# A feed-forward down projection in fp32 pieces: all block products written out, against seven block products for eight on part of it

## The chip, the cores and the metric

The kernel runs on one core of a Trainium2 chip. The metric is the time on the device of one execution of the whole layer, in microseconds (us), as the median of several runs. The engines are named as in the profile: PE (TensorE, matmuls), DVE (VectorE), ACT (ScalarE), POOL (GpSimd) and SP (SyncE, here only an issuer of transfers).

## The reference, cut to what matters

The layer is a mixer, a cross attention and a feed-forward block, each between norms. The change is in the last product of the last block.

```python
def swiglu_ffn(h, w_gate_up, w_down):
    g, u = jnp.split(h @ w_gate_up, 2, axis=-1)
    return (jax.nn.silu(g) * u) @ w_down          # (512 x 2816) @ (2816 x 1024), float32

...
        h = rms_norm(x, ffn_norm_pre[l])
        y = swiglu_ffn(h, w_gate_up[l], w_down[l])
        x = x + rms_norm(y, ffn_norm_post[l])
```

## The kernel before

Every fp32 product is made of three matmuls in a one-pass format (fp32r): each operand is parted into a rounded piece and the rest, and `mm3` (L285 to L288) adds low times high, high times low and high times high. `split` (L164 to L171) parts one operand: ACT copies it into the rounded piece (L166), then DVE, or POOL if it is named, subtracts that from the operand (L167).

A scheduler orders each engine's instructions after the program is written; pools give out buffers and make a later user wait for the last reader of the earlier one. SP issues the loads, in order.

The gate and up products (`gate_up`, L1338) run for eleven column blocks of 256, `d` = 0 to 10, and already use seven block products for eight: `Blocks.sums` (L1276) makes the sums of activations, DVE those of the weights. Before block 1 it first finishes the block 0 (L1373 to L1380). POOL multiplies the gated halves into `Gf[d]` (L1366, L1370), which holds 256 rows of the inner dimension for all 512 tokens.

The down product (L1387 to L1422) runs over 22 tiles `k` of 128 inner rows. For each, SP has loaded 128 x 1024 weights, two tiles to a transfer (L1393). ACT and POOL part the activations (`gs`), ACT and DVE the weights (`hi`, `lo`), and PE runs 24 matmuls of 128 x 512: four token tiles `i`, two column halves `n`, three pieces. The eight results stay in the eight banks `bk_ff`. Weights and activations share the eight buffers of the pool `fw`, three to a tile. The last six tiles (`LAST`) are parted ahead and kept in `wd` buffers, so that PE can finish one token tile after the other, while the norm, the residual and the store of the one before run beside it.

Of the kernel before, what the change touches and what calls it, by code (L numbers as in the profile page):

```python
# [47 lines left out]
def hybrid_layer(ctx, tc, a, out):  # L48
# [124 lines left out]
    def kview(w):  # L173
        return w.rearrange("(k p) c -> p k c", p=P)
# [1033 lines left out]
    def pool(name, bufs, side="left"):  # L1208
        return ctx.enter_context(tc.tile_pool(name=name, bufs=bufs, side=side, reuse_waits="tile"))
# [8 lines left out]
    def wtile(shape=(P, 4, 256), name="wc"):  # L1218
        return fw.tile(list(shape), F32R, tag="wc", name=name)
# [12 lines left out]
    def ntile(shape, name="xn"):  # L1232
        return fn.tile(shape, F32, tag="xn", name=name, bufs=2)

    def gtile(shape=(P, 2, 512), name="gf"):
        return fg.tile(list(shape), F32, tag="gf", name=name)

    class Blocks:
# [33 lines left out]

        def sums(self):  # L1276
            q, r = self.whole
            s = [gtile((P, 2, 4, 128), name="as") for _ in range(2)]
# [26 lines left out]
    def halves(t):  # L1305
        return t.rearrange("p (z t) -> p z t", z=2)
# [22 lines left out]
    late.close()  # L1329
    fraw.append(pool("fr1", 2))  # L1330
    fa.append(pool("fa1", 4))
    fg = pool("fg", NF // 2)
    ft = pool("ft", 1)
    A.take(fa[1], "S2", "S1", "S3", "S4")

    Gf = {}

    def gate_up(d):  # L1338

        glo, ghi, ulo, uhi = load_gu(d)  # L1340
        X, Y = bank("sc", "bk_X"), bank("d", "bk_Y")
        product(X, weights(glo), "11", True)
        x1 = etile(name="x1")
        nc.scalar.activation(x1, X, AF.Copy)
        w21 = weights(ghi, nc.vector if d == 1 else nc.gpsimd)
        t1 = ft.tile([P, 4, 256], F32, tag="t1", name="t1")
        nc.vector.tensor_tensor(t1, ulo, glo, op=OP.subtract)
        nc.vector.tensor_tensor(ulo, uhi, ulo, op=OP.subtract)
# [16 lines left out]
        Gf[d] = gtile()  # L1365
        nc.gpsimd.tensor_tensor(Gf[d][:, :, 0:256], halves(x1), halves(u2), op=OP.mult)  # L1366
# [24 lines left out]
    for g in range(NF // 2):  # L1391
        raw = fraw[1 - g // 2 % 2].tile([P, 2, D], F32, tag="raw", name="raw")
        nc.sync.dma_start(raw, wd[:, 2 * g:2 * g + 2, :])  # L1393
        for q in range(2):
            k = 2 * g + q
            gs = wtile((P, 2, 512), name="gs")
            if k >= NF - LAST:
                w2 = fa[len(tail) >= 3].tile([P, 2, D], F32R, tag="A", name="wd")
                hi, lo = w2[:, 0, :], w2[:, 1, :]
            else:  # L1400
                hi, lo = wtile((P, D), name="whi"), wtile((P, D), name="wlo")
            split(gs[:, 0], gs[:, 1], Gf[g][:, q], nc.gpsimd)
            split(hi, lo, raw[:, q, :])
            if k >= NF - LAST:
                tail.append((k, gs, hi, lo))
                continue
            for i in range(NT):
                t = slice(128 * i, 128 * i + 128)
                for n in range(2):
                    c = slice(512 * n, 512 * n + 512)  # L1410
                    mm3(bk[i][n], gs[:, 0, t], gs[:, 1, t], hi[:, c], lo[:, c], k == 0, False)
    for i in range(NT):
        t = slice(128 * i, 128 * i + 128)
        for n in range(2):
            c = slice(512 * n, 512 * n + 512)
            for k, gs, hi, lo in tail:
                mm3(bk[i][n], gs[:, 0, t], gs[:, 1, t], hi[:, c], lo[:, c], False, k == NF - 1)
        xo = ntile([P, D], name="xo")
        post_second(post_first(bk[i][0], g_post3, etile), bk[i][1], g_post3, res(i), xo, etile)
        for n in range(2):  # L1420
            c = slice(512 * n, 512 * n + 512)
            nc.sync.dma_start(out[0, 128 * i:128 * i + 128, c], xo[:, c])  # L1422
# [29 lines left out]
```

## Time and profile before

| what | value |
|---|---|
| median of 3 runs | 838.19 us (837.92 to 840.44) |
| the profiled execution, its own time | 842.27 us |
| span in its profile, first to last instruction | 840.5 us |
| PE busy, share of the span | 818.5 us, 97% |
| DVE, ACT, POOL busy | 535.3 us, 424.8 us, 290.8 us |
| mean granted clock of TensorE | 0.99 |

The span is what the profile's rows add up to; the profiled execution's own time is 1.8 us above it. The share of a busy engine is an average over stages with different limits, so that what matters is read from the stage of the change. Matmuls overlap in the record: one of 128 x 512 shows a length of 0.39 us, while the next starts 0.23 us later, and the distance from start to start is what a matmul costs.

### The profile page before, as it was taken

What the parts mean: (1) busy time and instruction counts of PE and PEld (TensorE: products, weight loads), DVE (VectorE), ACT (ScalarE), POOL (GpSimd) and SP (SyncE); (2) the same over time, 40 slices, a digit from 0 to 9 for tenths busy, and PEclk for the clock granted to TensorE, in tenths of its full rate; (3) what the DMA queues carried; (4) which work ended last, traced back from release to release, by engine and by line L of the source; (5) the groups of instructions that cost most, each with busy time, mean ns of one, the idle gap of its engine ahead of it and who ended that gap; (6) DMA issues with size and microseconds to landing.
All of it is one profiled execution on the core that took longest, in us unless ns stands there. A gap on an engine that the chain in (4) does not pass through costs nothing.

```text
span 840.5 us, 12639 instructions
## 1 busy us (share of the span) xinstructions
PE 818.5 (97%) x4838; PEld 706.2 (84%) x4838; DVE 535.3 (64%) x936; ACT 424.8 (51%) x840; POOL 290.8 (35%) x218
## 2 busy tenths in 40 slices
PE   8999989989999999999999999999999999999997
PEld 6877858876689878778888899999999999888885
DVE  5766684897889735743553779877888885124323
ACT  5535566768768643633543465444444444334311
POOL 1015331455537343501420101444444444323320
PEclk9999989999999999999999999999999999999999
DMA  8238312221102431243323034333333323222102
GB/s 249 75 106 259 110 52 81 82 70 63 63 14 89 150 102 51 100 150 101 101 101 100 10 117 152 119 109 106 114 103 103 102 101 101 101 101 100 51 26 76
DMA packets 67763, 83.18 MB, mean 99 GB/s; under 512 B 4368, under 2 KB 53873, under 8 KB 67702
## 3 DMA queue, kind: packets, MB, share of 16 engines
q1 hardware_dynamic: 64574, 77.97, 28.8%
q10 hardware_dynamic: 3128, 4.40, 1.7%
q8 instruction: 38, 0.62, 0.3%
q14 instruction: 23, 0.19, 0.1%
HBM read 80.24 MB, written 2.12 MB: 98 GB/s over the span
## 4 chain that ended last, share of the span: by engine, by line
PE 88%; DVE 7%; ACT 2%; issue 2%; DMA 1%; POOL 0%; SPq 0%; DVEq 0%; ACTq 0%; POOLq 0%
PE bk_dT L286 6%; PE bk_dT L287 6%; PE bk_dT L288 6%; PE bk_X L1300 5%; PE bk_X L1301 5%; PE bk_X L1302 5%; PE bk_ff L287 5%; PE bk_ff L288 5%; PE bk_ff L286 5%; PE bk_pv L1026 3%; PE bk_dN L287 3%; PE bk_dN L286 3%; PE bk_dN L288 3%; PE bk_Z L1300 2%; PE bk_Z L1301 2%; PE bk_Z L1302 2%
## 5 line engine op out<-in xcount | busy, mean ns | idle before, releaser
L166 ACT ACTIVATE whi<-raw 128x1024 fp32r<-128x1024 f32 (+1 forms) x80 | 76.8, 967 | 72.0 <-PE bk_dT L286 35.3
L167 DVE TENSOR_TENSOR wlo<-raw,whi 128x1024 fp32r<-128x1024 f32 x43 | 56.7, 1322 | 85.9 <-PE bk_ff L287 43.0
L167 POOL TENSOR_TENSOR wlo<-raw,whi 128x1024 fp32r<-128x1024 f32 x21 | 50.3, 2396 | 121.4 <-ACT whi L166 119.5
L166 ACT ACTIVATE wh<-raw 128x1024 fp32r<-128x1024 f32 x64 | 67.2, 1057 | 49.3 <-PE bk_X L1300 17.7
L167 POOL TENSOR_TENSOR wl<-raw,wh 128x1024 fp32r<-128x1024 f32 x19 | 55.4, 2917 | 97.3 <-ACT wh L166 69.9
L286 PE MATMUL bk_dT<-hTh,wlo 128*128 128x512 f32 x192 | 77.6, 404 | 1.2 <-DVE wlo L167 0.9
L287 PE MATMUL bk_dT<-hTl,whi 128*128 128x512 f32 x192 | 76.9, 400 | 0.0
L288 PE MATMUL bk_dT<-hTh,whi 128*128 128x512 f32 x192 | 76.4, 398 | 0.0
L167 DVE TENSOR_TENSOR wl<-raw,wh 128x1024 fp32r<-128x1024 f32 x45 | 65.7, 1465 | 9.3 <-ACT wh L166 9.3
L1301 PE MATMUL bk_X<-A,wh 128*128 128x256 f32 x192 | 54.5, 284 | 1.0 <-DVE A L167 1.0
L167 POOL TENSOR_TENSOR gs<-gf,gs 128x512 fp32r<-128x512 f32 x22 | 32.4, 1477 | 65.9 <-ACT gs L166 65.9
L1300 PE MATMUL bk_X<-A,wl 128*128 128x256 f32 x192 | 54.4, 283 | 0.4 <-ACT A L166 0.4
L1302 PE MATMUL bk_X<-A,wh 128*128 128x256 f32 x192 | 54.3, 283 | 0.0
L287 PE MATMUL bk_ff<-wlo,gs 128*128 128x512 f32 x128 | 49.8, 389 | 0.0
L288 PE MATMUL bk_ff<-whi,gs 128*128 128x512 f32 x128 | 49.6, 389 | 0.0
L1300 PE MATMUL bk_X<-AS,wl 128*128 128x256 f32 x160 | 45.6, 285 | 2.4 <-ACT u L1355 2.3
L286 PE MATMUL bk_ff<-whi,gs 128*128 128x512 f32 x128 | 47.4, 389 | 0.0
L996 POOL TENSOR_SCALAR s<-s,acf 128x128 f32<-128x128 f32 (+3 forms) x32 | 36.3, 1146 | 26.7 <-PE bk_tr L1011 15.9
L286 PEld LDWEIGHTS bk_dT<-hTh,wlo 128*128 128x128 f32 x192 | 36.6, 191 | 10.4 <-DVE wlo L167 2.1
L1302 PE MATMUL bk_X<-AS,wh 128*128 128x256 f32 x160 | 44.9, 281 | 0.0
L1300 PE MATMUL bk_Z<-AS,wl 128*128 128x256 f32 x160 | 44.9, 280 | 0.0
L1301 PE MATMUL bk_X<-AS,wh 128*128 128x256 f32 x160 | 44.8, 280 | 0.0
(376 smaller groups left out, 2527.9 us busy)
## 6 DMA issues: line engine op xcount, KB each, us to landing
raw<-in_w_gate_up_dram SPq DMA_DIRECT2D x22, 1024.0 KB, 5.5
raw<-in_w_down_dram SPq DMA_DIRECT2D x11, 1024.0 KB, 4.9
raw<-in_w_xkv_dram SPq DMA_DIRECT2D x8, 1024.0 KB, 5.3
raw<-in_w_in_dram SPq DMA_DIRECT2D x7, 1024.0 KB, 5.2
raw<-in_w_out_dram SPq DMA_DIRECT2D x4, 1024.0 KB, 5.0
raw<-in_w_xq_dram SPq DMA_DIRECT2D x4, 1024.0 KB, 5.2
raw<-in_w_xo_dram SPq DMA_DIRECT2D x4, 1024.0 KB, 5.0
raw<-in_w_in_dram SPq DMA_DIRECT2D x6, 512.0 KB, 4.8
```

Source lines behind the costliest of these rows:

```text
L166: first = nc.scalar.activation(hi, src, AF.Copy)
L167: second = (eng or nc.vector).tensor_tensor(lo, src, hi.bitcast(F32), op=OP.subtract)
L286: nc.tensor.matmul(o, lhsT=wl, rhs=xh, start=start, stop=False)
L287: nc.tensor.matmul(o, lhsT=wh, rhs=xl, start=False, stop=False)
L288: return nc.tensor.matmul(o, lhsT=wh, rhs=xh, start=False, stop=stop).ins
L996: ENG[on].tensor_scalar(s[:, 0:n], s[:, 0:n], c, None, op0=OP.mult)
L1026: nc.tensor.matmul(o, lhsT=v, rhs=pTs[br][q][:, j], start=(br, j, q) == mms[0], stop=(br, j, q) == mms[-1])
L1300: nc.tensor.matmul(o, lhsT=wl[:, k, c], rhs=A.hi(n, k), start=st, stop=False, skip_group_check=True)
L1301: nc.tensor.matmul(o, lhsT=wh[:, k, c], rhs=A.lo(n, k), start=False, stop=False, skip_group_check=True)
L1302: nc.tensor.matmul(o, lhsT=wh[:, k, c], rhs=A.hi(n, k), start=False, stop=stop and k == 3, skip_group_check=True)
```

## The change

The 2816 inner rows are seen as eleven pairs of tiles. Three pairs (`D0` = 3) are multiplied as before, into eight banks. For the other eight pairs the product is cut in two by two by two blocks: token halves 1 and 2, inner halves 1 and 2 (the two tiles of each pair), column halves 1 and 2. Seven block products replace eight: 11·11, 21·11, 12·21, 11·11, 12·22, 21·12 and 22·11 (activation block, weight block), where the blocks are overwritten in place by sums between the products. Each product takes four steps (`PAIRS`), and each step 12 matmuls of 128 x 512.

- The sums of activations (`gsum`) are eight DVE instructions of 128 x 1024.
- The first weight sum (11 += 12) is four DVE instructions (`wsum`, `dma=False`). The others (12 += 22, 11 += 22, 11 += 21) are twelve transfers of 512 KB, issued by POOL, which add what they read from the weights in memory onto a block that is already in the core (`accum_op=OP.add`).
- In the steps both lower pieces are made by DVE (before, POOL made those of the activations). `in_turn` keeps the order of the steps on ACT and DVE.
- Five additions of banks to kept results (`plus`, `kept`) are new, and the norm sums its halves as they come. Before the last product the rows 0 and 1 of token tiles are finished; only the rows 2 and 3 come after it.
- The activations of all blocks are now two tiles `G`, a part of which serves `sums` as its scratch.

```diff
-    wd = kview(a["w_down"][0])
-    bk = [[bank(t, "bk_ff") for t in ts] for ts in (("d", "d"), ("tr", "tr"), ("b", "b"), ("b", "b"))]
-    LAST = 6
...
-            split(gs[:, 0], gs[:, 1], Gf[g][:, q], nc.gpsimd)
-            split(hi, lo, raw[:, q, :])
...
-                    mm3(bk[i][n], gs[:, 0, t], gs[:, 1, t], hi[:, c], lo[:, c], k == 0, False)
...
+    def wsum(o, x, pairs, dma=True):
+        for q in pairs:
+            if dma:
+                last = nc.gpsimd.dma_start(block(o, *q), of_weights(x, *q), accum_op=OP.add)
+            else:
+                last = nc.vector.tensor_tensor(block(o, *q), block(o, *q), block(x, *q), op=OP.add)
+        return last.ins
+    def gsum(o, x, y, op, minus=False):
+        for q in FOURS:
+            o_, x_, y_ = (quarter(n, *q) for n in (o, x, y))
+            if minus:
+                nc.vector.scalar_tensor_tensor(o_, x_, -1.0, y_, op0=OP.mult, op1=op)
+            else:
+                nc.vector.tensor_tensor(o_, x_, y_, op=op)
+    def pieces(g, w, q, big=None):
...
+            wh, wl = wtile((P, 2, 512), name="whi"), wtile((P, 2, 512), name="wlo")
+        gs = wtile((P, 2, 2, 256), name="gs")
+        with in_turn():
+            split(gs[:, 0], gs[:, 1], quarter(g, *q))
+            parted.append(split(wh, wl, block(w, *q)))
+        return gs, wh, wl
...
+    def times(b, i, parts, q, start, stop):
+        gs, wh, wl = parts
+        t = slice(128 * i, 128 * i + 128)
+        for k in range(2):
+            d = q[0] + k
+            mm3s(b[i], gs[:, 0, k, t], gs[:, 1, k, t], wh[:, k], wl[:, k], start and d == D0, stop and d == ND - 1)
+    def one_pair(b, g, w, start, q):
+        parts = pieces(g, w, q)
+        for i in range(2):
+            times(b, i, parts, q, start, True)
...
+    c12, c22 = kept(X, pair_of("c12")), kept(Y, pair_of("c22"))
+    c21 = kept(V, [G[0][:, z, 0:2, :].rearrange("p d t -> p (d t)") for z in range(2)])
+    for q in PAIRS:
+        one_pair(X, "11", "11", True, q)
+        wsum("11", "12", [q], dma=False)
+    c11 = kept(X, pair_of("c11"))
+    gsum("21", "21", "22", OP.subtract)
+    last = wsum("12", "22", PAIRS[0:2])
+    for q in PAIRS:
+        one_pair(Y, "21", "11", True, q)
+        with tc.issue_after(last):
+            last = wsum("11", "22", [q])
+    plus(c22, Y)
+    gsum("11", "21", "11", OP.subtract)
+    with tc.issue_after(last):
+        last = wsum("12", "22", PAIRS[2:])
+    whole_product(Z, "12", "21", False)
+    plus(c11, Z)
+    whole_product(X, "11", "11", False)
+    plus(c12, X, OP.subtract)
+    gsum("21", "22", "11", OP.subtract, True)
+    gsum("12", "12", "11", OP.add)
+    with tc.issue_after(last):
+        wsum("11", "21", PAIRS)
+    whole_product(Y, "12", "22", False)
+    plus(c12, Y)
+    whole_product(X, "21", "12", False)
+    plus(c22, X, OP.subtract)
+    for i in range(2):
+        out_half(i, 1, c12[i], c12[i], True)
+        out_half(i, 0, c11[i], c11[i])
+        out_row(i)
+    TAIL = 2
...
+    for n, q in enumerate(PAIRS):
+        late = n >= len(PAIRS) - TAIL
+        parts = pieces("22", "11", q, fa[0] if late else None)
...
+    for i in range(2):
+        out_half(2 + i, 1, c22[i], c22[i], True)
+    for i in range(2):
+        for q, parts in tail:
+            times(X, i, parts, q, False, True)
+        nc.vector.tensor_tensor(c21[i], X[i], c21[i], op=OP.add)
+        out_half(2 + i, 0, c21[i], etile(name="yo"))
+        out_row(2 + i)
```

Three places of the order are needed below. The first is DVE in the down product. Before, from the last gate and up block on, its rows are the lower pieces of weights alone (`wlo`, and `wd` for the last six tiles):

```order
L1364 TENSOR_TENSOR u_7452<-u_7452,bk_Z 128x512
L167 TENSOR_TENSOR wlo<-raw,whi 128x1024 x10
L167 TENSOR_TENSOR wd<-raw,wd 128x1024 x2
L167 TENSOR_TENSOR wlo<-raw,whi 128x1024
L167 TENSOR_TENSOR wd<-raw,wd 128x1024 x2
```

With the change, these rows follow each other from the second step of the first block product to the first step of the second (`gs_7830` and `wlo_7829` are the second step's lower pieces, `gs_7898` and `wlo_7897` those of the second product's first; L1435 is a weight sum, L1444 a sum of activations):

```order
L167 TENSOR_TENSOR gs_7830<-gf_5118,gs_7830 128x512
L1435 TENSOR_TENSOR raw_7576<-raw_7576,raw_7578 128x1024
L167 TENSOR_TENSOR wlo_7829<-raw_7576,whi_7828 128x1024
L1444 TENSOR_TENSOR gf_5118<-gf_5119,gf_5118 128x1024
L167 TENSOR_TENSOR gs_7850<-gf_5118,gs_7850 128x512
L167 TENSOR_TENSOR wlo_7849<-raw_7582,whi_7848 128x1024
L1435 TENSOR_TENSOR raw_7576<-raw_7576,raw_7578 128x1024
L167 TENSOR_TENSOR gs_7870<-gf_5118,gs_7870 128x512
L167 TENSOR_TENSOR wlo_7869<-raw_7582,whi_7868 128x1024
L1435 TENSOR_TENSOR raw_7582<-raw_7582,raw_7580 128x1024
L167 TENSOR_TENSOR gs_7898<-gf_5119,gs_7898 128x512
L1444 TENSOR_TENSOR gf_5118<-gf_5119,gf_5118 128x1024
```

The next row is `wlo_7897`. Between the lower pieces of one step and the next now stand sums that the list before does not have.

The second place is DVE again, from the last step of the sixth product to the first of the seventh (`wlo_8282` and `wlo_8335`; L1522 finishes token row 1, L1491 takes the sixth product out of the bank into which the seventh adds):

```order
L167 TENSOR_TENSOR wlo_8282<-raw_7580,whi_8281 128x1024
L167 TENSOR_TENSOR gs_8336<-gf_5119,gs_8336 128x512
L1522 SCALAR_TENSOR_TENSOR xo_8318<-c12_7799,rs_r_8327,xin_113 128x512
L1522 SCALAR_TENSOR_TENSOR xo_8318<-c11_7889,rs_r_8327,xin_113 128x512
L167 TENSOR_TENSOR wlo_8335<-raw_7576,whi_8334 128x1024
L167 TENSOR_TENSOR gs_8355<-gf_5119,gs_8355 128x512
L1491 TENSOR_TENSOR c22_7802<-c22_7802,bk_ff_7592 128x512
```

Before, nothing read a bank in the middle of the down product; the finishing rows stood behind the last lower pieces.

The third is DVE between the gate and up blocks 0 and 1, as one piece of the difference (`A_4828` and `A_4829` are the lower pieces of the block 21 of the last token tile, in two halves, `A_4825` that of the block 22; L1279 to L1288 are sums of `Blocks.sums`, and `AS` their lower pieces):

```order
+L1279 TENSOR_TENSOR gf<-aw 128x512
+L1280 TENSOR_TENSOR gf<-gf,aw 128x512
+L1285 TENSOR_TENSOR aw<-aw 128x512
+L1288 TENSOR_TENSOR aw<-aw,gf 128x512
+L167 TENSOR_TENSOR AS_5114<-gf,AS_5114 128x4x128
+L167 TENSOR_TENSOR AS_5115<-gf,AS_5115 128x4x128
 L167 TENSOR_TENSOR A_4828<-bk_pn,A_4826 128x2x128
+L167 TENSOR_TENSOR AS_5116<-aw,AS_5116 128x4x128
+L1378 TENSOR_TENSOR gf<-s_5218,bk_Y 128x2x256
 L167 TENSOR_TENSOR A_4825<-bk_pn,A_4825 128x4x128
+L167 TENSOR_TENSOR AS_5117<-aw,AS_5117 128x4x128
 L167 TENSOR_TENSOR A_4829<-bk_pn,A_4827 128x2x128
```

Half of the sums, which stood behind the pieces of the last token tile, now stand ahead of and among them.

## Rows read from the trace of the kernel before

**Rows 1.** The page: the span, and busy time of each engine.

```profile
span 840.5 us, 12639 instructions
PE 818.5 (97%) x4838; PEld 706.2 (84%) x4838; DVE 535.3 (64%) x936; ACT 424.8 (51%) x840; POOL 290.8 (35%) x218
```

**Rows 2.** Busy time by stretch, and the columns.

```profile
core 0: us, PE busy (x) PEld busy (x) DVE busy (x) ACT busy (x) POOL busy (x), PEclk, DMA share, GB/s
711.00:834.40 123.40, 123.33 (x554) 101.85 (x552) 37.57 (x39) 37.69 (x57) 34.28 (x28) 1.00 0.21 73
500.00:700.00 200.00, 197.59 (x1645) 196.02 (x1645) 166.44 (x131) 98.41 (x124) 89.79 (x37) 1.00 0.32 106
```

**Rows 3.** Tile `bk_ff`: one of the three matmul rows of the first sixteen tiles.

```profile
L286 PE MATMUL bk_ff<-whi,gs x128: 387/389/398, 711.0 to 800.3; 128*128 128x512 f32 x128
```

**Rows 4.** Timeline of PE: starts of two matmuls of the down product, 19 steps apart.

```profile
738.65 0.39 PE L287 MATMUL bk_ff<-wlo,gs 128*128 128x512 f32 x1
...
742.95 0.39 PE L288 MATMUL bk_ff<-whi,gs 128*128 128x512 f32 x1
```

**Rows 5.** Waits in the down product, 710 to 800.5 us, longest first.

```profile
POOL gs L167 <- ACT gs L166: 59.1, 17, 6.4
DVE wlo L167 <- PE bk_ff L287: 43.0, 10, 8.2
```

**Rows 6.** Timeline of DVE: instructions that follow each other without a wait.

```profile
500.27 0.69 DVE L1281 TENSOR_TENSOR as<-as,aw 128x512 f32<-128x512 f32 x1
500.87 0.69 DVE L1286 TENSOR_TENSOR aw<-aw 128x512 f32<-128x512 f32 x1
...
517.35 3.43 DVE L167 TENSOR_TENSOR wl<-raw,wh 128x1024 fp32r<-128x1024 f32 x1
...
521.84 1.21 DVE L167 TENSOR_TENSOR wl<-raw,wh 128x1024 fp32r<-128x1024 f32 x1
522.98 1.21 DVE L1348 TENSOR_TENSOR raw<-raw 128x1024 f32<-128x1024 f32 x1
```

**Rows 7.** Timeline of POOL beside the longest of these.

```profile
516.31 3.39 POOL L167 TENSOR_TENSOR wl<-raw,wh 128x1024 fp32r<-128x1024 f32 x1 [27.36 <-DVE x L1351]
```

**Rows 8.** Timeline of ACT: one step's two upper pieces in the down product.

```profile
722.81 0.63 ACT L166 ACTIVATE gs<-gf 128x512 fp32r<-128x512 f32 x1 [4.38 <-PE bk_ff L288]
723.35 1.05 ACT L166 ACTIVATE whi<-raw 128x1024 fp32r<-128x1024 f32 x1
```

**Rows 9.** Timeline of PE: a matmul behind a wait, and the next two.

```profile
485.02 0.39 PE L1301 MATMUL bk_X<-A,wh 128*128 128x256 f32 x1 [0.97 <-DVE A L167]
485.24 0.28 PE L1302 MATMUL bk_X<-A,wh 128*128 128x256 f32 x1
485.36 0.28 PE L1300 MATMUL bk_X<-A,wl 128*128 128x256 f32 x1
```

**Rows 10.** Timeline of DVE and PE between gate and up blocks 0 and 1.

```profile
496.64 0.42 DVE L167 TENSOR_TENSOR A<-bk_pn,A 128x256 fp32r<-128x256 f32 x1 [2.64 <-ACT A L166]
...
498.13 0.28 PE L1300 MATMUL bk_X<-A,wl 128*128 128x256 f32 x1
```

**Rows 11.** Timeline of the end, from the last matmul on.

```profile
833.93 0.39 PE L288 MATMUL bk_ff<-wd,gs 128*128 128x512 f32 x1
834.36 0.60 ACT L259 ACTIVATE pn<-bk_ff 128x512 f32<-128x512 f32 x1 [3.39 <-PE bk_ff L288]
...
835.98 1.41 DVE L283 SCALAR_TENSOR_TENSOR xo<-yo,rs_r,xin 128x512 f32<-128x512 f32 x2 [0.20 <-POOL rs_r L280]
```

**Rows 12.** Transfers: KB of one, median us from issue to landing.

```profile
raw<-in_w_down_dram SPq DMA_DIRECT2D x11, 1024.0 KB, 4.9
raw<-in_w_in_dram SPq DMA_DIRECT2D x6, 512.0 KB, 4.8
xin<-in_x_dram SPq DMA_DIRECT2D x4, 512.0 KB, 3.6
raw<-in_w_in_dram SPq DMA_DIRECT2D x2, 304.0 KB, 7.7
```

More of the change, by code (lines that the diff above doesn't have):

```diff
@@ L1331, in hybrid_layer @@
     fa.append(pool("fa1", 4))
-    fg = pool("fg", NF // 2)
+    fg = pool("fg", 2)
     ft = pool("ft", 1)
     A.take(fa[1], "S2", "S1", "S3", "S4")
-    Gf = {}
+    G = [fg.tile([P, 2, NF // 2, 256], F32, tag="gf", name="gf") for _ in range(2)]
     def gate_up(d):
@@ L1412, in hybrid_layer @@
[L1412 to L1422, printed above, removed]
+    wd = a["w_down"][0].rearrange("(d h p) c -> p h d c", h=2, p=P)
@@ new lines, in hybrid_layer, with of_weights, load_b, load_plain @@
+    ND, D0 = NF // 2, 3
+    B = {}
+    def of_weights(name, d0, d1):
+        c = 512 * int(name[1]) - 512
+        return wd[:, int(name[0]) - 1, d0:d1, c:c + 512]
+    def load_b(name, g, home, tag):
+        t = B[name, g] = home.tile([P, 4, 512], F32, tag=tag, name="raw")
+        nc.sync.dma_start(t, of_weights(name, D0 + 4 * g, D0 + 4 * g + 4))
+    def load_plain(home):
+        raw = home.tile([P, 2, D], F32, tag="raw", name="raw")
+        nc.sync.dma_start(raw, wd[:, :, len(plain), :])
+        plain.append(raw)
@@ new lines, in hybrid_layer, with block, quarter @@
+    plain = []
+    load_plain(fraw[1])
+    load_plain(fraw[1])
+    load_plain(fraw[0])
+    load_b("11", 0, fraw[0], "raw")
+    load_b("12", 0, fa[0], "A")
+    load_b("12", 1, fa[0], "A")
+    load_b("11", 1, fa[1], "A")
+    load_b("21", 0, fa[1], "A")
+    load_b("21", 1, fa[1], "A")
+    load_b("22", 0, fa[1], "A")
+    load_b("22", 1, fraw[1], "raw")
+    def block(name, d0, d1):
+        g, k = (d0 - D0) // 4, (d0 - D0) % 4
+        return B[name, g][:, k:k + d1 - d0]
+    def quarter(name, d0, d1):
+        return G[int(name[0]) - 1][:, int(name[1]) - 1, d0:d1, :]
@@ new lines, in hybrid_layer, with in_turn @@
+    parted = []
+    def in_turn():
+        behind = ExitStack()
+        for ins in parted[-1] if parted else ():
+            behind.enter_context(tc.issue_after(ins))
+        return behind
+    def pieces(g, w, q, big=None):
+        if big:
+            W = big.tile([P, 2, 2, 512], F32R, tag="A", name="wd")
+            wh, wl = W[:, 0], W[:, 1]
+        else:
+            wh, wl = wtile((P, 2, 512), name="whi"), wtile((P, 2, 512), name="wlo")
[4 more added lines that the diff above has]
+        return gs, wh, wl
@@ new lines, in one_pair, with whole_product, plus, kept @@
+    def one_pair(b, g, w, start, q):
+        parts = pieces(g, w, q)
+        for i in range(2):
+            times(b, i, parts, q, start, True)
+    def whole_product(b, g, w, start):
+        for q in PAIRS:
+            one_pair(b, g, w, start, q)
+    def plus(t, b, op=OP.add):
+        for i in range(2):
+            nc.vector.tensor_tensor(t[i], t[i], b[i], op=op)
+    def kept(b, t):
+        for i in range(2):
+            nc.scalar.activation(t[i], b[i], AF.Copy)
+        return t
+    def pair_of(name):
+        return [etile(name=name) for _ in range(2)]
@@ new lines, in hybrid_layer, with out_half, out_row @@
+    outs, sq = {}, {}
+    def out_half(i, n, src, t, eps=False):
+        if i not in outs:
+            outs[i] = ntile([P, D], name="xo"), {}
+        xo, ts = outs[i]
+        sq[i, n] = small([P, 1], "ss%d" % n, 4)
+        square_sum(sq[i, n], src, xo[:, 512 * n:512 * n + 512])
+        if eps:
+            nc.vector.tensor_scalar(sq[i, n], sq[i, n], EPS, None, op0=OP.add)
+        nc.vector.tensor_tensor(t, src, g_post3[n], op=OP.mult)
+        ts[n] = t
+    def out_row(i):
+        xo, ts = outs[i]
+        e, r = small([P, 1], "rs_e", 4), small([P, 1], "rs_r", 4)
+        nc.gpsimd.tensor_tensor(e, sq[i, 0], sq[i, 1], op=OP.add)
+        nc.gpsimd.tensor_tensor(r, e, mhalf[:, 0:1], op=OP.pow)
+        for n in (1, 0):
+            c = slice(512 * n, 512 * n + 512)
+            nc.vector.scalar_tensor_tensor(xo[:, c], ts[n], r, res(i)[:, c], op0=OP.mult, op1=OP.add)
+            nc.sync.dma_start(out[0, 128 * i:128 * i + 128, c], xo[:, c])
@@ new lines, in hybrid_layer @@
+    X, Y, V, Z = ([bank(t, "bk_ff") for t in ts] for ts in (("d", "d"), ("tr", "tr"), ("b", "b"), ("b", "b")))
+    home = {"12": X, "22": Y, "21": V, "11": Z}
+    for d in range(D0):
+        ops = []
+        for z in range(2):
+            hi, lo = wtile((P, D), name="whi"), wtile((P, D), name="wlo")
+            gs = wtile((P, 2, 2, 256), name="gs")
+            with in_turn():
+                for u in range(2):
+                    split(gs[:, 0, u], gs[:, 1, u], G[u][:, z, d, :], nc.gpsimd if d else None)
+                parted.append(split(hi, lo, plain[d][:, z, :]))
+            ops.append((hi, lo, gs))
+        for zs in ((0,), (1,)) if d < D0 - 1 else ((0, 1),):
+            for name in ("12", "22", "21", "11"):
+                u, c = int(name[0]) - 1, 512 * int(name[1]) - 512
+                for i in range(2):
+                    t = slice(128 * i, 128 * i + 128)
+                    for z in zs:
+                        hi, lo, gs = ops[z]
+                        mm3s(home[name][i], gs[:, 0, u, t], gs[:, 1, u, t], hi[:, c:c + 512], lo[:, c:c + 512],
+                             d == z == 0, d == D0 - 1 and z == 1)
@@ L1425 @@
+    for i in range(2):
+        for q, parts in tail:
+            times(X, i, parts, q, False, True)
+        nc.vector.tensor_tensor(c21[i], X[i], c21[i], op=OP.add)
+        out_half(2 + i, 0, c21[i], etile(name="yo"))
+        out_row(2 + i)
 _INS = ['x', 'mem', 'rel_bias', 'mix_norm_pre', 'w_in', 'cmp_pos_k', 'cmp_pos_v', 'cmp_w1_k', 'cmp_w2_k', 'cmp_w1_v',
```

44 lines of the change are left out of this document (18 added, 26 removed).

## The prediction, made before the changed kernel was run

> **What bounds the kernel now.** I began with the page. The span is 840.5 us and PE is busy for 818.5 of it [rows 1], so PE bounds the kernel almost everywhere, and a matmul taken out is worth its time wherever PE does not start to wait. Then I read the down product by stretch: from 711.0 to 834.4 us PE is busy for 123.33 of 123.40 us, at the full granted clock (1.00, which is the 2.4 GHz level), while DVE, ACT and POOL have about 35 us of work each [rows 2]. Its matmuls are those of the down product (22 tiles of 24, 528, in three lines of which one has 128 for the first sixteen tiles [rows 3]) and the last of the gate's. The distance between starts gives the price: from 738.65 to 742.95 there are 19 steps of 0.226 us [rows 4]. The whole stage gives the mean: 24 gate matmuls of 0.12 us [rows 9] are 2.9, and (123.3 - 2.9)/528 = 0.228 us. The waits say how much room there was: in the down product DVE's lower pieces waited 43.0 us for PE to free a buffer, POOL's 59.1 us for ACT [rows 5]. Nobody waited on DVE. So the stage before is PE and nothing else, and the question is whether the other engines still keep up when DVE gets twice its work.
>
> **Fewer matmuls.** Three plain pairs are 3 x 48 = 144 matmuls, seven products of 4 steps of 12 are 336; together 480, 48 fewer: 48 x 0.228 = -10.9 us.
>
> **DVE's load in the steps.** A step gives PE 12 x 0.2265 = 2.72 us. From start to start, 512 elements on DVE take 0.60 and 1024 take 1.14 us [rows 6]; a scalar_tensor_tensor of 512 takes 0.70 (1.41 for two) [rows 11]. A step needs gs and wlo, 1.74 us; 28 steps are 48.7. To that come four weight sums (4.6), eight sums of activations (about 9.7), ten additions of banks (6.0) and the finishing of two rows (about 5): 74 us, against 28 x 2.72 = 76 us of PE. That is 97%, but no stall in itself: between 500 and 700 us DVE was busy 166 of 200 us and PE still 197.6 [rows 2]. What counts is where the work bunches, since the buffers let DVE run only about two steps ahead. ACT's two pieces of a step, about 0.55 + 1.0 [rows 8], fit into 2.72.
>
> **First bunch, products 1 to 2.** From the second step's gs to the second product's wlo, DVE's order has 4 gs (2.4), 4 wlo (4.56), 3 weight sums (3.4) and 2 sums of activations (2.3): 12.7 us. It can start about 0.2 us after PE enters product 1 (the buffers of the last plain pair are freed then), so wlo_7897 is ready 12.9 us in. PE wants it after four steps and one matmul, 10.9 + 0.2 = 11.1. Stall 1.8 us, and some 0.5 more in the next two steps, which have the remaining sum: **+2.3**. Its bounds: 0, if DVE gets half a step further ahead; 3.5, if DVE takes its whole 1.21 and 0.69 us per instruction, not the pitch.
>
> **Second bunch, start of product 7.** Its bank is read by L1491 first. Behind wlo_8282 stand gs, two L1522, wlo, gs and the first L1491: 0.60 + 1.4 + 1.14 + 0.60 + 0.68 = 4.4 us, while PE has about 2.5 us of its step left. Stall 1.9, and 0.2 for the second half-bank: **+2.1** (0 to 3).
>
> **Restarts.** The first matmul behind a wait costs more: 0.22 us to the next start where the next has 0.12 [rows 9]. About nine waits of this kind (products 1, 2 and 7): **+0.9** (0.3 to 1.5).
>
> **Gate and up, block 0 to 1.** DVE was idle for 2.64 us ahead of A [rows 10]; the four sums and two pieces now put there are 6 x 0.60 = 3.6 us, so it is 1.0 later. Two more pieces and L1378 (1.8) then stand ahead of A_4829; before, it was there by about 498.0 (PE goes on at 498.13), so it now comes at about 500.8. PE's first matmul with it stands 14 rows behind the one at 498.13, so at 498.13 + 14 x 0.12 = 499.8: **+1.0** (0 to 1.5). The hidden part is hidden by PE's own 14 matmuls alone.
>
> **The end.** Before, ACT squares the bank itself 0.43 us after the last matmul's start [rows 11]. Now a DVE addition (0.69) stands between: **+0.75**. The rest of the chain has the same length, and only two rows' finishing, not four, stands after the last product, as before one row.
>
> **The adding transfers.** Twelve of 512 KB, issued by POOL; no row of before shows one. The nearest rows are loads of 512 KB by SP: 3.6 and 4.8 us, and of 1024 KB (as an addition also reads what it changes): 4.9; the slowest kind took 7.7 for 304 KB [rows 12]. They go one after another by their blocks: the first can start about 3 us into product 1, the last is needed about 73 us in, before product 7's last step. So they are hidden up to 70/12 = 5.8 us each; beyond that each further us costs 12. I take 4.8, like the 512 KB loads of weights: hidden, **0**. Bounds 3.6 (0) and 7.7 (+22). The Trainium skill, "DMA: Bandwidth & Descriptors", section on the anatomy of one DMA on the gpsimd path, gives 2.0 us + bytes/436e3 for such a transfer; my estimate from it is 3.2 us, so by that too the sum stays the same. No run here shows it yet. The loads themselves (8 of 1 MB for the blocks, three for the plain pairs) are the 11 of before and go through the same queue, whose share of the engines was 0.21 [rows 2].
>
> **Sum.** -10.9 + 2.3 + 2.1 + 0.9 + 1.0 + 0.75 = -3.85. The span goes from 840.5 to 836.6, and with the 1.8 around it the execution from 842.27 to 838.4. The profiled execution stood 4.1 us above the median of 838.19; I take that off and forecast a median of **834.3**. By the terms' bounds without the transfers it is 829 to 838. What this measurement can tell from no change is 0.3%, so under 835.7 is faster and over 840.7 slower.
>
> **Rivals.**
> *The adding transfers are too slow.* From 6.4 us each (12 x 6.4 - 70 = 6.8 us of waits, more than the 6.4 that separate forecast and bound), the kernel is slower; 6.5 us gives 842, 7.7 gives 856. For it: an addition has to read as much again, and small loads took up to 7.7. Against it: 1 MB loads in the same stage took 4.9, and the engines are 80% idle [rows 2, 12]. ACT's upper pieces in product 4 or 7 would wait for a transfer. Chance 0.18.
>
> *DVE becomes the bound.* At 1.21 and 0.69 per instruction its 74 us are 79 to 80, above PE's 76, and what PE loses grows by about 3 us to 837.5 (836 to 841). For it: only three per cent of room. Against it: the rows show the pitch held over instructions that follow each other, and the steps are such instructions. Chance 0.14.
>
> *POOL and DVE hold each other up.* One DVE lower piece of 1024 took 3.43 us instead of 1.21 where a POOL lower piece took 3.39 at the same time [rows 6, 7]. If writing out a transfer did the same to DVE, twelve times 2.2 us = 26 us would fall on an engine with 2 us of room: 855 to 860. Against it: POOL no longer makes pieces in the steps, which is the one thing that the row shows to collide; issuing a transfer moves no tile through POOL. Chance 0.05. The Trainium skill, "SBUF — State Buffer", section "Who interferes with whom", has a DVE instruction with two inputs from SBUF contend with a GpSimd one that reads it, and holds (as an inference) that writing descriptors is not stopped by it; with the first the rows agree. By its "DVE blocks DMA" trap a DVE instruction of another kind does stop it: if it held here, the first four transfers would wait for DVE's first pause, about 22 us into product 1, and the limit of 5.8 us would fall to 4.2, at which 4.8 us each would cost 7 us: 841. It is inside this chance.
>
> *The stalls are absent.* If PE never waits in the steps or between the blocks: -10.9 + 0.9 + 0.75, 829. For it: DVE was idle 70% of the stage and PE waited for nobody [rows 2]. Against it: the counts above, which hold at any start. Chance 0.08.
>
> **How the numbers follow.** The forecast has what is left, 0.55, with a range of its own of 831 to 837.5. Of it some 0.5 lies under 835.7; with the absent stalls and the lower part of the dear DVE, faster has 0.60. Same has 0.17 (the upper edge of the forecast, most of the dear DVE), slower 0.23 (transfers 0.18, collisions 0.05). The range of 829 to 846 leaves out the slow end of the transfers, the collisions and half of the absent stalls, together under 0.2.
>
> **What would show it.** 480 matmuls on `bk_ff`, 0.226 to 0.23 from start to start. PE's longest waits on DVE's wlo at the first step of product 2 (near 1.8 us) and on L1491 at the first of product 7 (near 2). DVE's rows 1.14 and 0.60 apart; if they are dearer, or stretched where POOL issues, the second or third rival holds. Transfers that land in under 5.8 us one after another, and no piece of ACT waiting for one; if ACT waits, it is the first rival. A wait of about 1 us of PE near 499.8 us, and 0.75 us more from the last matmul to the end. Wrong it would be above all through the price of an adding transfer, which nothing here shows.

## The result

The changed kernel takes 846.33 us (median of 5 runs, 844.47 to 849.37) against 839.66 us of the kernel before (5 runs): 1.0092 times, 95% interval 1.0075 to 1.0109. It is 6.7 us slower, where 3.9 us less had been forecast, and just above the upper end of the range (846). Its profiled execution has this page (to read beside [rows 1]):

```profile
span 845.3 us, 12704 instructions
PE 807.3 (96%) x4790; PEld 694.6 (82%) x4790; DVE 584.2 (69%) x1004; ACT 449.4 (53%) x878; POOL 280.8 (33%) x216
```

PE has 48 matmuls and 11.2 us of work less, as counted. So the time went into waits. Busy time by stretch of the down product (columns as in [rows 2]) shows where:

```profile
core 0: us, PE busy (x) PEld busy (x) DVE busy (x) ACT busy (x) POOL busy (x), PEclk, DMA share, GB/s
747.00:758.00 11.00, 11.00 (x47) 8.49 (x48) 11.00 (x12) 7.21 (x10) 2.65 (x2) 1.00 0.40 55
758.00:770.00 12.00, 11.01 (x48) 8.37 (x47) 12.00 (x14) 6.82 (x9) 2.42 (x2) 1.00 0.53 85
...
802.00:813.00 11.00, 9.37 (x42) 7.42 (x40) 5.63 (x9) 8.17 (x15) 2.44 (x2) 1.00 0.50 81
813.00:836.00 23.00, 14.84 (x54) 11.38 (x55) 14.61 (x22) 4.61 (x8) 3.46 (x5) 0.78 0.37 88
```

In products 1 and 2 (747 to 770 us) DVE is busy all the time, and PE nearly so. The loss comes from about 811 us on, in the last step of the sixth product: PE stands, DVE stands too (5.63 of 11 us busy), and TensorE's granted clock is down, 0.78 on the mean of the stretch.

The chain can be followed from PE back. PE's timeline there:

```profile
820.93 1.19 PE L1469 MATMUL bk_ff<-whi,gs 128*128 128x512 f32 x2 [9.57 <-DVE gs L167]
...
822.57 0.63 PE L1471 MATMUL bk_ff<-whi,gs 128*128 128x512 f32 x1
823.00 0.63 PE L1469 MATMUL bk_ff<-whi,gs 128*128 128x512 f32 x1
...
826.33 0.47 PE L1469 MATMUL bk_ff<-whi,gs 128*128 128x512 f32 x1 [0.23 <-DVE c L1491]
```

PE waits 9.57 us for a lower piece, and then starts matmuls 0.43 us apart (822.57 to 823.00) where it had 0.226: that is the lower of the clock's two levels, 1.2 in place of 2.4 GHz. The granted clock was 1.00 up to 815 us and 0.50 from 816 to 825 us, so it fell during the standstill. The matmul at 820.93 begins a step of twelve, and the 48 of the seventh product follow from 826.33 on, where L1491 frees the bank; so the wait lies at the end of product 6. (The expectation of e1 below puts it into the last product.) DVE's timeline says why the piece (820.10) is late:

```profile
804.82 0.15 DVE L1511 TENSOR_SCALAR ss<-ss 128x1 f32<-128x1 f32 x1
...
806.68 1.22 DVE L167 TENSOR_TENSOR wlo<-raw,whi 128x1024 fp32r<-128x1024 f32 x1
818.11 1.41 DVE L1522 SCALAR_TENSOR_TENSOR xo<-c,rs_r,xin 128x512 f32<-128x512 f32 x2 [10.21 <-POOL rs_r L1519]
...
820.10 0.68 DVE L167 TENSOR_TENSOR gs<-gf,gs 128x512 fp32r<-128x512 f32 x1
```

It stood behind the finishing of row 0 (L1522), which waited 10.21 us for a column of 128 numbers from POOL. And POOL's timeline:

```profile
804.13 1.22 POOL L1433 DMA_DIRECT2D raw<-in_w_down_dram  x1 [4.73 <-issue]
809.96 1.21 POOL L1433 DMA_DIRECT2D raw<-in_w_down_dram  x1 [4.61 <-ACT gs L166]
815.99 1.22 POOL L1433 DMA_DIRECT2D raw<-in_w_down_dram  x1 [4.82 <-issue]
816.75 0.68 POOL L1518 TENSOR_TENSOR rs_e<-ss,ss 128x1 f32<-128x1 f32 x1
817.51 0.56 POOL L1519 TENSOR_TENSOR rs_r<-rs_e,mhalf 128x1 f32<-128x1 f32 x1
```

Each adding transfer holds POOL's own queue for about 6 us (the twelve start from 748.92 to 815.99, 6.1 apart): 1.2 us of work and 4.8 of standing, one transfer after the other, also where no semaphore is awaited ("issue"). By the landings in the trace, each of the eleven later ones starts 0.26 to 0.32 us after the one before has landed. The two small operations of row 0 (L1518 and L1519, under 1 us each) are queued behind the twelfth, though their input was there near 805 us (L1511 of DVE).

Two smaller losses lie outside. Between the gate and up blocks and in one of them PE waits:

```profile
498.92 0.39 PE L1300 MATMUL bk_X<-A,wh 128*128 128x256 f32 x1 [1.03 <-DVE A L167]
...
644.15 0.36 PE L1299 MATMUL bk_X<-AS,wl 128*128 128x256 f32 x1 [1.36 <-ACT u L1355]
```

The first had been forecast. The second is DVE's, ahead of ACT's `u`:

```profile
635.70 3.39 POOL L167 TENSOR_TENSOR wl<-raw,wh 128x1024 fp32r<-128x1024 f32 x1
636.74 3.43 DVE L1444 TENSOR_TENSOR gf<-gf 128x1024 f32<-128x1024 f32 x1
```

One of the eight sums of activations had been ordered into the gate and up stage, fell beside a lower piece of POOL, and took 3.43 us, as the piece in [rows 6, 7] had. Before, L1348 stood in its place and took 3.31 us there; now L1348 comes behind the sum, with 1.21. The end is the other:

```profile
837.15 0.39 PE L1471 MATMUL bk_ff<-wd,gs 128*128 128x512 f32 x1
...
837.74 0.19 POOL L1518 TENSOR_TENSOR rs_e<-ss,ss 128x1 f32<-128x1 f32 x1 [16.54 <-ACT xo L259]
838.00 0.55 POOL L1519 TENSOR_TENSOR rs_r<-rs_e,mhalf 128x1 f32<-128x1 f32 x1
839.10 0.60 POOL L1518 TENSOR_TENSOR rs_e<-ss,ss 128x1 f32<-128x1 f32 x1 [0.54 <-ACT xo L259]
839.78 0.94 POOL L1519 TENSOR_TENSOR rs_r<-rs_e,mhalf 128x1 f32<-128x1 f32 x1
```

The last row's two small operations take 0.60 and 0.94 us, the ones before 0.19 and 0.55: they run while DVE finishes row 2 (L1522, from 838.91 on), and the ones before begin while DVE reads a bank (L1596).

**Three stages.** From here on each profile is cut at three starts: of the first gate matmul, of the first down matmul and of the last. What lies ahead of the first of them is the same work in all kernels, and took 477.6 to 483.9 us in their profiles, whatever the kernel. This spread of 6 us is wider than most differences between the medians, and the stages are free of it; but each row's stages are those of one profiled execution. In us:

| kernel | gate and up | down, to the last matmul's start | end | sum | median, ratio to before (interval) |
|---|---|---|---|---|---|
| before | 227.4 | 122.9 | 6.6 | 357.0 | 839.4 to 840.1 |
| changed | 229.6 | 126.4 | 8.1 | 364.2 | 846.33, 1.0092 (1.0075 to 1.0109) |
| e1_rows_late | 229.9 | 118.4 | 10.9 | 359.2 | 841.65, 1.0025 (1.0009 to 1.0042) |
| e2_no_transfers | 230.0 | 117.0 | 8.1 | 355.1 | 838.37, 0.9991 (0.9977 to 1.0006) |
| e3_copies | 230.1 | 118.5 | 8.2 | 356.7 | 837.83, 0.9983 (0.9962 to 1.0005) |
| e4_half | 229.5 | 118.4 | 8.2 | 356.1 | 839.58, 0.9988 (0.9972 to 1.0004) |
| e5_split_transfers | 229.5 | 118.5 | 8.2 | 356.2 | 836.67, 0.9960 (0.9945 to 0.9974) |
| e9_copies_272 | 229.7 | 117.0 | 8.1 | 354.8 | 837.59, 0.9976 (0.9961 to 0.9991) |
| e12_half_columns | 229.5 | 165.0 | 8.2 | 402.7 | 887.81, 1.0568 (1.0550 to 1.0587) |
| e6_bank_first | 229.7 | 114.3 | 9.4 | 353.4 | 836.75, 0.9961 (0.9947 to 0.9975) |
| e8_all | 227.1 | 114.1 | 9.4 | 350.6 | 833.54, 0.9924 (0.9907 to 0.9941) |
| e7_sums_moved | 227.2 | 114.3 | 9.4 | 350.9 | 832.11, 0.9910 (0.9895 to 0.9925) |
| e10_row1_early | 227.8 | 114.1 | 8.2 | 350.1 | 833.50, 0.9916 (0.9896 to 0.9935) |

### The profile page after: what moved, and what is told of

Its sections match the earlier page's. It is cut to its first block, busy times and chain, and to the rows that moved or that the text cites. A ratio compares the mean times of both kernels' runs of the same rounds, so it can differ in the third digit from the quotient of the medians.

```text
span 845.3 us, 12704 instructions
## 1 busy us (share of the span) xinstructions
PE 807.3 (96%) x4790; PEld 694.6 (82%) x4790; DVE 584.2 (69%) x1004; ACT 449.4 (53%) x878; POOL 280.8 (33%) x216
## 4 chain that ended last, share of the span: by engine, by line
PE 80%; DVE 9%; issue 5%; ACT 2%; POOL 2%; DMA 1%; DVEq 0%; ACTq 0%; POOLq 0%; SPq 0%
PE bk_dT L286 5%; PE bk_dT L287 5%; PE bk_dT L288 5%; PE bk_X L1299 5%; PE bk_X L1300 5%; PE bk_X L1301 5%; PE bk_pv L1026 3%; PE bk_ff L1470 3%; PE bk_ff L1469 3%; PE bk_ff L1471 3%; PE bk_dN L287 3%; PE bk_dN L286 3%; PE bk_dN L288 3%; PE bk_Z L1299 2%; PE bk_Z L1300 2%
## 5 line engine op out<-in xcount | busy, mean ns | idle before, releaser
L166 ACT ACTIVATE whi<-raw 128x1024 fp32r<-128x1024 f32 (+1 forms) x96 | 93.5, 981 | 71.7 <-PE bk_dT L286 31.6
L167 DVE TENSOR_TENSOR wlo<-raw,whi 128x1024 fp32r<-128x1024 f32 x59 | 74.9, 1271 | 60.7 <-ACT whi L166 35.0
L167 POOL TENSOR_TENSOR wl<-raw,wh 128x1024 fp32r<-128x1024 f32 x19 | 53.5, 2818 | 100.4 <-ACT wh L166 100.4
L1469 PE MATMUL bk_ff<-whi,gs 128*128 128x512 f32 x152 | 53.6, 397 | 9.8 <-DVE gs L167 9.6
L1470 PE MATMUL bk_ff<-wlo,gs 128*128 128x512 f32 x152 | 60.9, 401 | 1.0 <-DVE wlo L167 1.0
L1471 PE MATMUL bk_ff<-whi,gs 128*128 128x512 f32 x152 | 59.8, 395 | 0.0
L166 ACT ACTIVATE gs<-gf 128x512 fp32r<-128x512 f32 (+1 forms) x40 | 21.9, 565 | 44.6 <-PE bk_ff L1471 37.9
L1300 PE MATMUL bk_Z<-AS,wh 128*128 128x256 f32 x160 | 44.8, 280 | 0.0
L1301 PE MATMUL bk_Z<-AS,wh 128*128 128x256 f32 x160 | 44.8, 280 | 0.0
```

Of the source, the lines that this page charges most:

```text
L166: first = nc.scalar.activation(hi, src, AF.Copy)
L167: second = (eng or nc.vector).tensor_tensor(lo, src, hi.bitcast(F32), op=OP.subtract)
L1300: nc.tensor.matmul(o, lhsT=wh[:, k, c], rhs=A.lo(n, k), start=False, stop=False, skip_group_check=True)
L1301: nc.tensor.matmul(o, lhsT=wh[:, k, c], rhs=A.hi(n, k), start=False, stop=stop and k == 3, skip_group_check=True)
L1469: nc.tensor.matmul(b, lhsT=gl, rhs=wh, start=start, stop=False, skip_group_check=True)
L1470: nc.tensor.matmul(b, lhsT=gh, rhs=wl, start=False, stop=False, skip_group_check=True)
```

## The experiments

All start from the changed kernel unless said otherwise.

### Who stands in whose queue: e1_rows_late and e2_no_transfers

e1 moves the finishing of rows 0 and 1 from ahead of the last product to behind its last lower pieces (`in_turn` now also keeps the activations' pieces in order):

```diff
-        out_row(i)
...
+    with in_turn():
+        for i in range(2):
+            out_row(i)
```

> Rows 0 and 1 are finished (POOL's two small operations, VectorE's last two, the store) behind the last lower pieces instead of ahead of the last product's; all else is as in the changed kernel, the twelve adding transfers too. Theory A (VectorE stood behind POOL's small operations, and these behind the transfers in POOL's queue): PE's wait of 9.6 us at the second step of the last product goes, and with it the slow clock behind it; what is left is a wait of some 3 to 5 us for the twelfth transfer, which still lands near 821.7 us, so 837 to 841 us. Theory B (VectorE has too much work in the steps, and the queue is only where it shows): the wait comes back at another row of VectorE, 844 to 848 us.

The down stage falls from 126.4 to 118.4 us: the 9.6 us wait is gone, although the twelve transfers still go 6.2 us apart and end as late. The longest wait left in the last product is 2.5 us for L1491 (the second bunch of the prediction). PE does not wait for the twelfth sum, so the 3 to 5 us that I had put aside for it are not there. The end grows to 10.9 us in return: ACT's squares for the rows 2 and 3 now wait for the stores of rows 0 and 1 (5.8 us in two waits), so that the time is 841.65 us, just above what theory A had.

e2 leaves the transfers out:

```diff
             if dma:
-                last = nc.gpsimd.dma_start(block(o, *q), of_weights(x, *q), accum_op=OP.add)
+                continue
```

> The twelve adding transfers are left out, so that three of the weight sums are missing from the result; every other row stays. Theory A: nothing stands ahead of POOL's small operations and no piece waits for a transfer; what is left are the waits that were foreseen at products 1 to 2 and at the start of product 7 (about 2 us each) and the longer end: 833 to 836 us. Theory B: PE still waits 8 us or more for VectorE in product 7, 843 to 848 us.

Down 117.0 us, as theory A says; the median, 838.37 us, is 2.4 us above the band that I gave; in its profile the gate and up stage and the end are longer than in my sum, by 1.6 and 0.8 us. Its waits in the down product (PE's, then those of its weight loads):

```profile
PE bk_ff L1469 <- DVE c L1491: 2.6, 1, 2.6
...
PE bk_ff L1470 <- DVE wlo L167: 1.0, 1, 1.0
...
PEld bk_ff L1470 <- DVE wlo L167: 3.5, 8, 1.4
```

These are the two forecast bunches, and PE waits for nothing else. Theory B, that DVE's load would bring the long wait back, falls with both runs.

### What holds POOL: e3_copies, e4_half, e9_copies_272, e5_split_transfers, e12_half_columns

e3 takes `accum_op=OP.add` away; e4 adds only the first tile of each pair (`q[0]` to `q[0] + 1`); e9 copies columns 0 to 383 alone.

> The twelve transfers copy instead of adding (the three weight sums are so replaced by one addend); same bytes written, same queue. If the addition makes a transfer long, they follow each other in under 4 us in place of 6.06, POOL is free before 800 us, and the time is that of the kernel without transfers, 833 to 836 us. If writing a transfer out to POOL's queue does it, the distance stays near 6 us and the time at 844 to 848 us.

> Each adding transfer adds only the first of its two tiles (256 KB; half of each sum is missing from the result). If a transfer's price goes with its bytes, the distance falls to about 3.3 us, POOL is free before product 7, and the time is 833 to 836 us. If it is a fixed price for each transfer, the distance stays above 5 us and the time above 843 us.

> The twelve transfers copy instead of adding, and only columns 0 to 383 of each tile (384 KB; the three weight sums are so replaced by something else), which breaks each partition's row in two: 272 packets where the whole copies had 144. Theory Q1: one at a time again, 4.5 to 6 us apart, and POOL is free only at 800 to 817 us: 839 to 848 us. Theory Q2 (it is the addition): as the whole copies, several on their way at once, POOL free before 795 us, 836 to 840 us.

In all three POOL is free by 788 us and the down stage is 117.0 to 118.5 us. So it is neither the addition alone (e4 adds) nor the size alone (e3 moves as many bytes). The medians of e3 and e4 (837.83 and 839.58 us) are above their bands of 833 to 836, as e2's is. What these have in common is in the record of the queue: packets, MB, share of the engines, then KB of one and median us to landing. Of the changed kernel, and under it of e3:

```profile
q0 software_dynamic: 3264, 6.29, 4.6%
raw<-in_w_down_dram POOLq DMA_DIRECT2D x12, 512.0 KB, 5.8
```

```profile
q0 software_dynamic: 1728, 6.29, 2.3%
raw<-in_w_down_dram POOLq DMA_DIRECT2D x12, 512.0 KB, 4.2
```

A transfer is 272 packets in the changed kernel, 144 in e3 and e4. e9 was to have 272 without an addition, but its record has 112 (1344 in all): it did not test what it was made for. Two more kernels, both adding all that the changed one adds, do. e5 (the first addition below) parts each transfer by tiles, with rows of 2 KB, e12 (the second) by columns, with rows of 1 KB:

```diff
-                last = nc.gpsimd.dma_start(block(o, *q), of_weights(x, *q), accum_op=OP.add)
+                for d in range(*q):
+                    last = nc.gpsimd.dma_start(block(o, d, d + 1), of_weights(x, d, d + 1), accum_op=OP.add)
...
+                for c in (slice(0, 256), slice(256, 512)):
+                    last = nc.gpsimd.dma_start(block(o, *q)[:, :, c], of_weights(x, *q)[:, :, c], accum_op=OP.add)
```

> Each adding transfer of 512 KB becomes two of 256 KB, one for each of its two tiles; the same bytes are added, nothing is left out. Theory Q1 (POOL's queue holds only so many packets at a time: one transfer of 272 packets, or three of 144, and POOL stands until an earlier one has landed): up to three are on their way, the 24 follow each other in about 1.4 to 2 us, POOL is free before 800 us and the time is that of the kernel without transfers, 836 to 840 us. Theory Q2 (the added bytes have a price of their own, some 6 us for 512 KB): two halves take as long as a whole, 843 to 848 us.

> The changed kernel with each adding transfer as two of 256 KB, parted by columns, not by tiles: half the bytes each, but rows of 1 KB, so 272 packets each as the whole had. Nothing is left out. Theory Q1 (packets fill POOL's queue): one at a time, 24 of some 4.5 to 6 us each, so that product 4 and all behind it wait for sums: 860 to 890 us. Theory Q3 (bytes fill it, or the count of transfers): three at a time as the halves by tile, 836 to 842 us.

Both issue 24 transfers of 256 KB. Queue and POOL's timeline of e5, then of e12:

```profile
q0 software_dynamic: 3456, 6.29, 4.9%
raw<-in_w_down_dram POOLq DMA_DIRECT2D x24, 256.0 KB, 5.1
...
766.37 0.87 POOL L1434 DMA_DIRECT2D raw<-in_w_down_dram  x1 [0.67 <-issue]
768.06 0.87 POOL L1434 DMA_DIRECT2D raw<-in_w_down_dram  x1 [0.81 <-issue]
769.93 0.89 POOL L1434 DMA_DIRECT2D raw<-in_w_down_dram  x1 [1.00 <-issue]
```

```profile
q0 software_dynamic: 6528, 6.29, 5.0%
raw<-in_w_down_dram POOLq DMA_DIRECT2D x24, 256.0 KB, 4.3
...
756.25 1.23 POOL L1434 DMA_DIRECT2D raw<-in_w_down_dram  x1 [3.23 <-issue]
760.95 1.21 POOL L1434 DMA_DIRECT2D raw<-in_w_down_dram  x1 [3.47 <-issue]
765.29 1.22 POOL L1434 DMA_DIRECT2D raw<-in_w_down_dram  x1 [3.13 <-issue]
```

With 144 packets each (e5) the starts in these rows are 1.7 to 1.9 us apart and a transfer lands after 5.1: three are on their way, and from the eighth on each starts 0.30 to 0.32 us after the third before it has landed. With 272 (e12) they are 4.3 to 4.7 us apart and land after 4.3: one, and each starts 0.26 to 0.32 us after the one before has landed. The same bytes in the same number of transfers cost 887.81 us or 836.67. e12 loses most of it at the place of the changed kernel's wait, behind POOL's 24th transfer, and most of the rest in product 4, whose pieces wait for sums:

```profile
PE bk_ff L1470 <- DVE gs L167: 30.7, 1, 30.7
...
DVE xo L1523 <- POOL rs_r L1520: 31.8, 2, 31.3
```

Theory Q1 holds in these runs: of transfers with 144 packets three may be on their way, of those with 272 one, and POOL stands until an earlier one has landed. Theories Q2 and Q3 fall. How many entries there are, and of what, stays open: three of 144 go together, two of 272 do not, and in e9 a fourth of 112 waited as well. If packets are counted, there is room for 3 x 144 = 432 and not for 4 x 112 = 448, which is an estimate from these runs. All additions of 272 packets write two rows in each partition and those of 144 one; no run separates the rows from the packets.

The Trainium skill, "DMA: Bandwidth & Descriptors", section "SWDGE vs HWDGE vs iDMA", says that GpSimd itself computes the descriptors of such transfers and appends them to rings in SBUF, and that only one queue of this kind is allocated. That POOL is held until an earlier transfer has landed is not on the page, and is what these runs show; that the rings are full then is not shown. By the same page's section on the anatomy of such a DMA my estimate had been 3.2 us for 512 KB; the trace has 4.2 for a copy and 5.8 for an addition, and the measurement decides.

### Giving the other terms back: e6, e8, e7, e10

e6 is e5 with another order on DVE in the last product (`pieces` takes a row behind which its lower pieces are issued, `lows` holds the lower pieces made so far):

```diff
-    plus(c22, X, OP.subtract)
+    done = plus(c22, X, OP.subtract)
...
-        out_row(i)
+    out_row(0)
...
-        parts = pieces("22", "11", q, fa[0] if late else None)
+        parts = pieces("22", "11", q, fa[0] if late else None, done if n else None)
...
+    with tc.issue_after(lows[-1]), tc.issue_after(lows[-2]):
+        out_row(1)
```

> As the one with 24 halves, and VectorE's order at the last product is changed: the two additions that take the sixth product out of its bank come right behind the first step's lower pieces, the finishing of row 1 and the halves of rows 2 and 3 behind all lower pieces. If PE's 2.6 us wait at the start of product 7 is this order and nothing else, it falls under 1 us and the time is 2 to 3 us under that of the halves alone, 834 to 837 us. If VectorE simply has too much work there, the wait comes back at a lower piece and the time stays at 836 to 840 us.

The down stage falls by 4.2 us, from 118.5 to 114.3; no wait over 0.3 us is left at product 7, and the low clock that e5 had behind its wait there is gone with it (some 1.4 of the 4.2; e2 and e9 had the wait without it). The end takes 1.2 of it back (9.4 us). The medians of e5 and e6 do not differ (4 and 6 runs, which scatter over 1.8 and 4.3 us), so this gain rests on the stages of one profile each.

e8 is e6 with three moves more: the first weight sum by eight more transfers of 256 KB, the sums of activations for product 2 beside the plain pairs (`gsum` under `in_turn()` in the loop over `d`, at `d == 0`), and `A.sums()` behind the last token tile's pieces (`tc.issue_after`). e7 is e8 without the first of these.

> As the one before, and three moves more: the first weight sum by eight adding transfers of 256 KB too (VectorE has no weight sums left); the sums of activations for the second product beside the plain pairs, none within the gate and up stage; the sums between gate and up blocks 0 and 1 behind the pieces of the last token tile, as before the change. If the waits at products 1 to 2 (2.2 us) are VectorE's load there, and the 1.0 and 1.1 us lost in the gate and up stage are those two placements, the time is 3 to 4 us under that of the one before, 830 to 834 us. If more transfers crowd POOL's queue, ACT waits for one in product 2 and the time is 835 to 842 us.

> As the kernel with all moves, but the first weight sum is VectorE's again (24 transfers of 256 KB, not 32). If ACT's 11 us of waits for the eight extra transfers cost that kernel what VectorE had won, this one is 1 to 2 us under it, 831 to 833 us, with no ACT wait for a transfer in products 1 to 4. If VectorE's load in products 1 to 2 binds in spite of the sums of activations moved away, PE waits there 1 to 2 us and the time is the same, 833 to 835 us.

In both the gate and up stage is back at 227.1 and 227.2 us (before: 227.4): the two placements are what it had lost. The down stage stays at 114.1 and 114.3. In e8 DVE's relief in products 1 and 2 was eaten by waits of ACT for the extra transfers:

```profile
ACT whi L1467 <- DMA raw<-in_w_down_dram: 11.0, 7, 2.1
```

In e7 those waits are gone, and PE has the 1.0 us wait of the changed kernel at the first step of product 2 again, so that neither of its two theories is decided. The bunch there holds the same rows as in the changed kernel: the sums that were moved stood ahead of it already, one in the gate and up stage and one in the plain pairs.

> As the one before, and row 1 is finished ahead of the last two lower pieces, not behind all. In the kernel with all moves the square of row 3 waited 7.4 us for the store of row 1 (its scratch is that row's buffer), and VectorE stood 2.5 us behind it at the end. If that wait makes the end longer (9.4 us from the last matmul on, against 8.2), the end comes back to about 8.2 us and the time is 1 us under the one before, 830 to 832.5 us. If the lower pieces come too late instead, PE waits 1 to 2 us in the last product and the time is 832 to 835 us.

e10 finishes row 1 ahead of the last two lower pieces. ACT no longer waits for the store (7.4 us in e7), and the end is back at 8.2 us, with the down stage the same (114.1). The sum of stages is the lowest of all, 350.1 us; the median, 833.50 us, is not: it lies in the band of the other theory, though PE has no such wait. e7, e8 and e10 can't be told apart by their intervals. All three beat both kernels: 0.991 to 0.992 of the time before.

## Why the prediction was wrong

**Fewer matmuls, the two bunches, restarts: right.** The sum was -10.9 + 2.3 + 2.1 + 0.9 = -5.6 us; without the transfers the down stage falls by 5.9 (122.9 to 117.0). The longest waits stand where they were forecast, at the first step of product 2 (1.0 us on PE and more in its weight loads, for 1.8) and at product 7's start (2.6 for 1.9). From start to start, products 1 and 2 of e2 take 11.65 and 12.47 us where an undisturbed one takes 10.88, 2.4 us together; product 7 starts 2.9 us late. That is 5.3 us, as the three terms add up to.

**The adding transfers: this step failed.** I wrote "So they are hidden up to 70/12 = 5.8 us each ... I take 4.8, like the 512 KB loads of weights: hidden, 0". They came 6.1 us apart, which is inside the bounds and by that formula costs 12 x 6.1 - 70 = 3.2 us. They cost 9.4 (126.4 against 117.0): the wait of 9.6 and some 2.3 of low clock behind it, less some 2.5, since product 7's own wait for L1491 shrank from 2.6 to 0.2. In e1, where they come 6.2 us apart, PE does not wait for any of them. So the size was off, but the mechanism was the error: I asked when ACT needs the last sum, and not what else stands in POOL's queue. POOL had been idle for most of the stage [rows 2] and I treated it as free, but POOL, which only had to issue the transfers, was held by each of them, and the finishing of rows 0 and 1 has two operations in it for each row. Behind those of row 0 stood DVE's L1522, which I had counted as work and not as a wait, behind that the lower pieces of product 6's last step, and behind those PE. The order is fixed before a run, so POOL's and DVE's lists could have shown this; what I had written out of DVE's begins behind that row, and of POOL's there is nothing. e1 takes only this apart and gets 8.0 of the 9.4 us back; the other 1.4 is what it loses to the low clock behind its 2.5 us wait, and e3 to e5 lose the same there with no transfer in the way.

**The rivals.** The one that I gave 0.18, transfers too slow, had the sign and nearly the place, but not the mechanism: ACT did wait for the eleventh and twelfth sum (7.7 us), and PE did not wait for them. DVE's rows in the steps kept 1.14 and 0.60 us from start to start. POOL's writing of a transfer did not hold DVE: its pieces took 1.22 and 0.68 us beside it. The "DVE blocks DMA" trap of the Trainium skill's page "SBUF — State Buffer" is about DVE instructions of another kind; had it held here too, DVE would have held POOL. While DVE was busy 11.00 of 11.00 us (747 to 758), POOL's transfers took their 1.2 to 1.4 us, as later with an idle DVE (1.21 at 809.96), so for these two-input instructions the trace agrees with the page's inference that they do not. The stalls were not absent either.

**Gate and up, block 0 to 1: right, but not all.** The forecast +1.0 is there (1.03 us at 498.92). The stage lost 2.2, since a sum of activations had been ordered into a gate and up block as well (PE's wait of 1.36 us at 644.15, where none was over 0.3 before). I had read DVE's order only at the places where I expected the change.

**The end: too small.** +0.75 was forecast, +1.5 came. The addition is there; besides, POOL's last two small operations take 0.8 us longer, beside DVE's finishing of row 2, as "Who interferes with whom" on the same page has it for a DVE instruction with two inputs from SBUF and a GpSimd one that reads it.

With the measured terms the sum is -5.9 + 9.4 + 2.2 + 1.5 = +7.2 us, which is the difference of the stages (364.2 - 357.0); the medians differ by 6.7.

## What to carry to other kernels

When a change gives an engine that was idle something to issue, list what else stands in that engine's queue behind it, and who waits for that; the bandwidth of the transfers is the second question. A transfer issued by POOL can hold it until an earlier one has landed, so cut it into transfers of few packets, and keep small operations on the path out of that queue or ahead of it. More transfers make more waits for them (e8). Compare kernels by stages, from the same matmul on, where the stages ahead scatter by more than the effect.

## What was not expected of the hardware

- An adding transfer of 512 KB (272 packets) and one of 256 KB with rows of 1 KB (272 packets) go one at a time, 6.1 and 4.6 us apart; of 144 packets three go together. A copy of 512 KB has 144 packets where the addition has 272.
- After PE's waits of 2.5 to 2.6 us in the last product the granted clock fell in some profiles (e1, e3, e4, e5: some seven matmuls 0.43 us apart, about 1.4 us lost) and not in others (e2, e9). What decides it is not shown.
- POOL's operation on 128 numbers took 0.19 us beside a DVE instruction that reads a bank and 0.60 beside L1522. In e6 it took 4.04 us: five DVE instructions with two inputs from the core's memory ran beside it one after another, the last of which ended at 814.54 us, and it ended then (e10: 4.05). In e2, e3 and e5 it took 2.91 beside four. With DVE idle it took 0.68 us, right behind a transfer (816.75 in the changed kernel). So a small operation on POOL can be held by DVE's work as well as by POOL's queue. POOL's row of e6 and DVE's last of the five:

```profile
810.54 4.04 POOL L1525 TENSOR_TENSOR rs_e<-ss,ss 128x1 f32<-128x1 f32 x1 [2.78 <-DVE ss L1517]
...
813.32 1.22 DVE L1468 TENSOR_TENSOR wlo<-raw,whi 128x1024 fp32r<-128x1024 f32 x1
```
